# A Strassen-like combination moved one unit later in the MLP's last eighth but one

## The chip, the cores and the metric

The kernel runs on one core of a Trainium2 chip. Its time is the device time of one execution in microseconds, and the number compared is the median over several runs.

Five engines take part, each with a queue of its own that runs in order: TensorE (PE in the profile, with its weight loads as PEld), VectorE (DVE), ScalarE (ACT), GpSimd (POOL) and SyncE (SP). Matmuls write to accumulator banks in PSUM. VectorE and ScalarE read those banks, and a bank can be written for the next result once its last reader is done.

## The reference

A trunk of two layers on 256 positions of width 2048. Each layer is a mixing block (attention and gating) and then an MLP; the change lies in the MLP.

```python
for l in range(DEPTH):                       # DEPTH = 2
    ...                                      # norm, input projection, attention and gating, output projection, residual
    h2 = rms_norm(x, norm2_g[l])
    x = x + jnp.square(jax.nn.relu(h2 @ w_up[l])) @ w_down[l]     # 2048 -> 8192 -> 2048
return rms_norm(x, final_g)
```

## The kernel before

**Precision.** Weights are split: `hi` is the weight rounded to the faster matmul type (a copy on ScalarE, L167), `lo` the rest (a subtraction on VectorE, L177). Activations are split in the same way (`half`, `hs`, `shared`). A product is three matmuls: hi by hi, lo by hi, hi by lo (L400, L402, L404). The weights stream from memory in blocks of 128 x 1024; one block is one *unit*: one load by SP into a `raw` buffer (7 of them), one `hi` (6 buffers), one `lo` (6 buffers), and 24 matmuls on PE.

**Order.** A list `steps` holds the work of PE in order, written out by hand; the main loop goes through it and counts units in `done` (`now` in the helpers). At each step it first issues the `hi` for the unit five places ahead, then what has come due, then the `lo` for the unit four places ahead, then loads, and then the step's matmuls; what follows a finished column (`after`) is issued behind them. `soon(n, fn)` makes a piece of work due n units after the unit at which it is called. So a number in `soon` sets at which place of every engine's queue the work stands, and nothing reorders it later.

**The MLP.** The 8192 hidden columns are worked in eighths, e = 0 to 7. Round e of the loop (e = 0 to 8) holds the up projection of eighth e (16 units, result in `inner` and `half`) and the down projection of eighth e − 1. Part of the down projection's columns is done in groups of 512 by `fast`, a scheme of seven products in place of eight (Strassen's) over 2 x 2 blocks; each `fast` step counts as four units. The seven sums of a group gather over the eighths, and at the group's last round `combine` makes the four result blocks from them. The first group (g = 0, columns 0 to 511 of the output) keeps its seven sums in the four `aux` banks of PSUM over all rounds, but the seventh's earlier part, which is stored in memory and read back by POOL (L877).

For group 0, `combine(stage, 0, ..., o)` is issued in round 7, which is the last eighth but one of the down projection. It consists of:
- a copy of the first sum on ScalarE (L813),
- eight adds and subtractions of 128 x 256 on VectorE (L814 to L819, L821, L822), which read the aux banks,
- three units later four scalings on ScalarE (L827, in `scale`),
- six and seven units later two sets of four transposes on PE (L839, in `turn_back`), each followed one unit later by an add to the residual x on VectorE (L499, in `update`).

**The stretch around it.** Below, D0 to D7 are the eight units of the ordinary down projection in round 7. They do column pairs 8, 10, 12 and 14 (blocks of 128 columns), two units each. In this round the units use two banks in turn, `acc0` and `acc1`: pair 10 (D2, D3) and pair 14 (D6, D7) both use `acc0`, pairs 8 and 12 `acc1`. After pair 10 is finished, two operations on VectorE free `acc0`: L761 multiplies the bank by the norm factors in place, L499 adds it to x. E0 to E15 are the units of round 8, the last eighth's down projection, with all four banks.

The calls are counted from the unit n of group 0's second `fast` step in round 7. Up units follow at n + 4 to n + 10, D0 to D7 at n + 11 to n + 18, E0 at n + 19. `combine` at n + 14 is issued at D3, the unit before pair 10's `after`.

```python
LAST = (4, 6, 8, 10, 0, 2, 12, 14)          # L65: order of the column pairs in round 8
soon(17 + 2 * i, lambda c=c: rest_in(c))    # L880: pairs 12 and 14 into x, at D6 and E0
```

Of the kernel before, what the change touches and what calls it, by code (L numbers as in the profile page):

```python
# [90 lines left out]
def trunk(ctx: ExitStack, tc: tile.TileContext, layout, xT, consts, gains, w, b_sp, w_sp, out):  # L91
# [23 lines left out]
    stage, stage_one = ar[:, 2048:3840], ar[:, 3840:4096]  # L115
# [130 lines left out]
    def soon(delay, fn):  # L246

        due.append((now[0] + delay, fn))
# [258 lines left out]
    def layer(l, n1, n2, n3, last):  # L507
# [261 lines left out]
        def rest_in(c):  # L769
            y = rest_sums[:, c - 12:c - 10, :]  # L770
            vec.tensor_tensor(y, y, wide(n2.R2), op=OP.mult)
            vec.tensor_tensor(x[:, c:c + 2, :], x[:, c:c + 2, :], y, op=OP.add)
# [35 lines left out]
        def combine(place, c, banks, o=None):  # L808

            d1, d2, d3, d5, d7, d6, d4 = (place[:, 256 * n:256 * (n + 1)] for n in range(7))  # L810
            p1, p2, p3, p5, p7, p6, p4 = o or (d1, d2, d3, d5, d7, d6, d4)
            if o:
                act.activation(d1, p1, AF.Copy)  # L813
            vec.tensor_tensor(d2, d1, p2, op=OP.add)  # L814
            vec.tensor_tensor(d6, d1, p6, op=OP.add)
            vec.tensor_tensor(d7, d6, p7, op=OP.add)
            vec.tensor_tensor(d6, d6, p5, op=OP.add)
            vec.tensor_tensor(d3, d6, p3, op=OP.add)
            vec.tensor_tensor(d4, d7, d4, op=OP.subtract)  # L819
            if o:  # L820
                vec.tensor_tensor(d4, d4, p4, op=OP.subtract)  # L821
            vec.tensor_tensor(d7, d7, p5, op=OP.add)  # L822

            def scale():
                for tt, out in enumerate(((d2, d3), (d4, d7))):
                    for d in out:
                        act.activation(d, d, AF.Copy, scale=n2.r2[:, tt:tt + 1])  # L827

            soon(3, scale)
            wait = 6 if o else 7  # L830
            soon(wait, lambda: turn_back(c, d2, d4, banks[0]))
            soon(wait + (1 if o else 2), lambda: turn_back(c + 2, d3, d7, banks[1]))

        def turn_back(c, first, second, bank):
            ps = bank()
            for j in range(2):
                for tt, src in enumerate((first, second)):
                    o = j * S + tt * P
                    pe.transpose(ps[:, o:o + P], src[:, j * P:(j + 1) * P], ident)  # L839
            soon(1, lambda: update(n3, c, ps, False, last))  # L840
# [27 lines left out]
        def seventh_out(e, o):  # L868
            act.activation(stage_one, o[6], AF.Copy)  # L869
            put(e, 0, slice(0, 256))  # L870

        def first_done(e):
            def f(o):
                if e < 7:
                    soon(5, lambda: seventh_out(e, o))
                else:
                    soon(10, lambda: nc.gpsimd.dma_start(stage[:, 1536:1792], far[0]))  # L877
                    soon(14, lambda: combine(stage, 0, [aux_bank] * 2, o))
                    for i, c in enumerate((12, 14)):
                        soon(17 + 2 * i, lambda c=c: rest_in(c))  # L880
            return f
# [186 lines left out]
```

## Time and profile before

| | |
|---|---|
| median of 3 runs | 2035.05 us (2034.97 to 2035.65) |
| span of the profiled execution, first to last instruction | 2033.3 us |
| median less that span | 1.75 us |
| TensorE busy | 2018.3 us (99%) |
| VectorE busy | 1577.6 us (78%) |
| ScalarE busy | 1213.4 us (60%) |
| GpSimd busy | 156.7 us (8%) |
| memory traffic over the span | 205 GB/s |

For the profiled execution the profile gives the span and no other time; what lies around it is taken from the median. Times inside are microseconds from the span's start. A timeline row reads: start, duration, engine, line of the kernel, operation, output<-input, shapes, count, and in brackets the idle time of that engine just before it with what ended it. Where an instruction waits for several things, the profile names the one that came last; if that one had nothing to do with it, the true cause is another that came at about the same time.

### The profile page before, as it was taken

The numbers are of one execution on the slowest core, as the hardware profiler recorded it, in microseconds if no ns is written. First come the engines' busy times: TensorE is split into PE (matmuls) and PEld (weight loads), VectorE is DVE, ScalarE is ACT, GpSimd is POOL, SyncE is SP. The second block draws the span as 40 slices with busy tenths as digits, with TensorE's granted clock in tenths as the row PEclk, the third lists the DMA queues.
The fourth block names the chain that finished last, engine by engine and source line by source line (L and its number), as shares of the span: only waits on it lengthen the run. The fifth ranks groups of instructions, "written<-read, shape, count | busy, mean of one in ns | idle before, by whom it ended". The sixth has DMA issues, their size and how long they took to land.

```text
span 2033.3 us, 40721 instructions
## 1 busy us (share of the span) xinstructions
PE 2018.3 (99%) x16834; PEld 1979.1 (97%) x16834; DVE 1577.6 (78%) x1950; ACT 1213.4 (60%) x1613; POOL 156.7 (8%) x200
## 2 busy tenths in 40 slices
PE   9999999999999999999999999999999999999997
PEld 8998999999999999999989989999999999999997
DVE  7566766688888898998856667667888898888985
ACT  7565454666666666656545654556666666667654
POOL 0002300000001001100000032000000100010000
PEclk9999999999999999999999999999999999999998
DMA  8555556566677766875664555565676776778562
GB/s 326 192 167 166 187 187 205 169 232 209 211 228 236 244 218 201 243 222 198 204 214 159 169 184 187 187 203 179 215 223 213 230 234 217 230 221 261 184 213 81
DMA packets 126443, 419.27 MB, mean 206 GB/s; under 512 B 14128, under 2 KB 22064, under 8 KB 126256
## 3 DMA queue, kind: packets, MB, share of 16 engines
q1 hardware_dynamic: 110800, 389.86, 56.4%
q0 software_dynamic: 14304, 23.86, 6.7%
q8 instruction: 132, 2.16, 0.4%
q10 hardware_dynamic: 1152, 2.94, 0.4%
q14 instruction: 55, 0.45, 0.1%
HBM read 394.58 MB, written 22.02 MB: 205 GB/s over the span
## 4 chain that ended last, share of the span: by engine, by line
PE 95%; DVE 3%; ACT 1%; issue 1%; DMA 1%; ACTq 0%; DVEq 0%; SPq 0%
PE acc L402 23%; PE acc L400 23%; PE acc L404 23%; PE acc L461 3%; PE acc L460 3%; PE acc L459 3%; PE aux L430 3%; PE aux L432 3%; PE acc L433 3%; PE aux L433 3%; PE acc L432 3%; PE acc L430 3%; DVE lo L177 1%; ACT hi L167 1%; PE aux L693 0%
## 5 line engine op out<-in xcount | busy, mean ns | idle before, releaser
L167 ACT ACTIVATE hi<-raw 128x1024 fp32r<-128x1024 f32 (+1 forms) x817 | 836.2, 1051 | 497.9 <-DVE raw L219 231.2
L177 DVE TENSOR_TENSOR lo<-raw,hi 128x1024 fp32r<-128x1024 f32 (+1 forms) x817 | 964.1, 1213 | 155.1 <-ACT hi L167 151.7
L400 PE MATMUL acc<-hs,hi 128*128 128x256 f32 x2816 | 781.3, 277 | 0.0
L402 PE MATMUL acc<-hs,lo 128*128 128x256 f32 x2816 | 779.4, 277 | 0.2
L404 PE MATMUL acc<-hs,hi 128*128 128x256 f32 x2816 | 778.3, 276 | 0.0
L402 PEld LDWEIGHTS acc<-hs,lo 128*128 128x128 f32 x2816 | 528.7, 188 | 2.5 <-DVE lo L177 1.8
L400 PEld LDWEIGHTS acc<-hs,hi 128*128 128x128 f32 x2816 | 528.7, 188 | 0.3 <-issue 0.2
L404 PEld LDWEIGHTS acc<-hs,hi 128*128 128x128 f32 x2816 | 528.6, 188 | 0.0
L400 PE MATMUL acc<-half,hi 128*128 128x256 f32 x1344 | 372.1, 277 | 2.3 <-ACT hi L167 2.3
L402 PE MATMUL acc<-half,lo 128*128 128x256 f32 x1344 | 371.0, 276 | 0.0
L404 PE MATMUL acc<-half,hi 128*128 128x256 f32 x1344 | 371.0, 276 | 0.0
L400 PEld LDWEIGHTS acc<-half,hi 128*128 128x128 f32 x1344 | 252.3, 188 | 2.6 <-ACT hi L167 2.6
L402 PEld LDWEIGHTS acc<-half,lo 128*128 128x128 f32 x1344 | 252.3, 188 | 0.0
L404 PEld LDWEIGHTS acc<-half,hi 128*128 128x128 f32 x1344 | 252.2, 188 | 0.0
L866 POOL DMA_DIRECT2D far<-ar x92 | 74.7, 983 | 1159.9 <-ACT ar L869 607.0
L432 PE MATMUL acc<-lo,shared 128*128 128x256 f32 x384 | 106.4, 277 | 0.0
L433 PE MATMUL acc<-hi,shared 128*128 128x256 f32 x384 | 106.1, 276 | 0.0
L430 PE MATMUL acc<-hi,shared 128*128 128x256 f32 x384 | 106.1, 276 | 0.0
L459 PE MATMUL acc<-hi,hs 128*128 128x512 f32 x256 | 101.5, 397 | 0.1
L461 PE MATMUL acc<-hi,hs 128*128 128x512 f32 x256 | 100.6, 393 | 0.0
L460 PE MATMUL acc<-lo,hs 128*128 128x512 f32 x256 | 100.1, 391 | 0.3 <-DVE lo L177 0.3
L643 DVE TENSOR_TENSOR half<-ar,half 128x512 fp32r<-128x512 f32 x72 | 49.7, 691 | 62.1 <-ACT half L640 61.0
(163 smaller groups left out, 2560.2 us busy)
## 6 DMA issues: line engine op xcount, KB each, us to landing
raw<-in_w SPq DMA_DIRECT2D x731, 512.0 KB, 4.7
far<-ar POOLq DMA_DIRECT2D x60, 256.0 KB, 6.0
far<-ar POOLq DMA_DIRECT2D x32, 128.0 KB, 4.5
ar<-far POOLq DMA_DIRECT2D x12, 256.0 KB, 8.6
raw<-in_w SPq DMA_DIRECT2D x10, 256.0 KB, 5.2
x<-in_xT SPq DMA_DIRECT2D x7, 256.0 KB, 5.6
out<-x SPq DMA_DIRECT2D x7, 256.0 KB, 3.1
shared<-in_b_sp ACTq DMA_DIRECT2D x2, 512.0 KB, 7.8
```

What stands on the lines that cost most here:

```text
L167: act.activation(self.h[:, j * m:(j + 1) * m], self.raw[:, j * m:(j + 1) * m], AF.Copy)
L177: vec.tensor_tensor(lo[:, r], self.raw[:, r], self.h[:, r].bitcast(F32), op=OP.subtract)
L400: pe.matmul(o, lhsT=hi, rhs=xs[:, 0, :], start=(k0 + k == 0 and (two or cb == 0)), stop=False, skip_group_check=True)
L402: pe.matmul(o, lhsT=wt.lo[:, k, cb * P:(cb + 1) * P], rhs=xs[:, 0, :], start=False, stop=False, skip_group_check=True)
L404: pe.matmul(o, lhsT=hi, rhs=xs[:, 1, :], start=False, stop=last, skip_group_check=True)
L430: pe.matmul(o[n], lhsT=xh, rhs=hi, start=(p == 0 and k == 0 and n in fresh), stop=False, skip_group_check=True)
L432: pe.matmul(o[n], lhsT=xh, rhs=lo, start=False, stop=False, skip_group_check=True)
L433: pe.matmul(o[n], lhsT=xl, rhs=hi, start=False, stop=(n in last and p == 1 and k == 1), skip_group_check=True)
L459: pe.matmul(ps, lhsT=xh, rhs=hi, start=(k0 + k == 0), stop=False)
L460: pe.matmul(ps, lhsT=xh, rhs=lo, start=False, stop=False)
L461: pe.matmul(ps, lhsT=xl, rhs=hi, start=False, stop=(k0 + k == KC - 1))
L866: nc.gpsimd.dma_start(far[g][:, r], src, **({} if e == max(g, 1) else {"accum_op": OP.add}))
```

## The change

One number in `first_done`: the combination of group 0 comes due at 15 units after n, in place of 14. This holds for both layers.

```diff
                 else:
                     soon(10, lambda: nc.gpsimd.dma_start(stage[:, 1536:1792], far[0]))
-                    soon(14, lambda: combine(stage, 0, [aux_bank] * 2, o))
+                    soon(15, lambda: combine(stage, 0, [aux_bank] * 2, o))
                     for i, c in enumerate((12, 14)):
                         soon(17 + 2 * i, lambda c=c: rest_in(c))
```

It is now issued at D4, behind the `after` of pair 10. Its scalings, transposes and adds are due relative to it and move by one unit as well.

VectorE's queue in layer 0 around the combination, the earlier file's rows with − and the changed one's with +. The names in it: `aux` are the banks of the seven sums, `ar` the place where they are combined, `acc_11479` the bank `acc0` with pair 10.

```order
 L643 TENSOR_TENSOR shared<-ar,shared 128x2x256 x2
+L177 TENSOR_TENSOR lo<-raw,hi 128x1024
+L761 TENSOR_TENSOR acc_11479<-acc_11479,nR_3824 128x512
+L499 TENSOR_TENSOR x<-x,acc_11479 128x512
 L814 TENSOR_TENSOR ar<-ar,aux 128x256
 L815 TENSOR_TENSOR ar<-ar,aux 128x256
```

Further down in the same queue, at the end of the eight operations:

```order
 L821 TENSOR_TENSOR ar<-ar,aux 128x256
 L822 TENSOR_TENSOR ar<-ar,aux 128x256
-L177 TENSOR_TENSOR lo<-raw,hi 128x1024
-L761 TENSOR_TENSOR acc_11479<-acc_11479,nR_3824 128x512
-L499 TENSOR_TENSOR x<-x,acc_11479 128x512
 L177 TENSOR_TENSOR lo<-raw,hi 128x1024 x2
```

One `lo` (for D7) and the two operations that free `acc0` have passed from behind the eight operations to ahead of them; the next two `lo` (for E0 and E1) stand behind all of it as before.

ScalarE's queue at the same place, with the copy L813 and the four scalings L827:

```order
 L640 ACTIVATE shared<-ar 128x2x256 x2
-L167 ACTIVATE hi<-raw 128x1024
+L167 ACTIVATE hi<-raw 128x1024 x2
 L813 ACTIVATE ar<-aux 128x256
 L167 ACTIVATE hi<-raw 128x1024 x3
 L827 ACTIVATE ar<-ar,nr_3823 128x256 x4
-L167 ACTIVATE hi<-raw 128x1024 x3
+L167 ACTIVATE hi<-raw 128x1024 x2
 L285 ACTIVATE hs<-x,cols 128x256 x2
```

The copy and the scalings both stand one `hi` conversion later. On PE the two sets of transposes stand ahead of E2 and E3 where they stood ahead of E1 and E2; on VectorE the add of the first set moves behind one more `lo`, and that of the second behind one more `lo` and the work of the next finished pair. The queues of POOL and SP keep their order.

## The prediction

> **What bounds the kernel now.** I read the page's first two parts first, to see which engine sets the time.
>
> ```profile
> span 2033.3 us, 40721 instructions
> PE 2018.3 (99%) x16834; PEld 1979.1 (97%) x16834; DVE 1577.6 (78%) x1950; ACT 1213.4 (60%) x1613; POOL 156.7 (8%) x200
> PEclk9999999999999999999999999999999999999998
> ```
>
> TensorE is busy for 99% of the span at full clock until the last slice. Anything that doesn't make PE wait is therefore free, and a change that moves no matmul in number can only win what PE loses in waits. So the next view was the list of waits with PE as the one that waits (line waited for, total us, times, longest), and the one line of the weight loads' list that names VectorE's low halves in the MLP.
>
> ```profile
> PE acc L400 <- ACT hi L167: 2.3, 2, 1.1
> PE aux L321 <- DVE nr L347: 1.2, 1, 1.2
> PE aux L986 <- DVE warm L982: 1.1, 1, 1.1
> PE acc L460 <- DVE lo L177: 0.3, 1, 0.3
> PEld acc L402 <- DVE lo L177: 1.8, 8, 0.3
> ```
>
> The largest entry happens twice, once per layer. L321 is the final norm, L986 the start; neither is near the change. The eight L402 waits are at most 0.3 us each. The two L400 waits lie in these stretches (busy time and count by engine, then granted clock, DMA share, GB/s):
>
> ```profile
> 960.00:970.00 10.00, 8.86 (x79) 8.69 (x78) 9.86 (x13) 4.87 (x8) 0.00 (x0) 1.00 0.58 177
> 970.00:980.00 10.00, 10.00 (x91) 10.00 (x90) 8.52 (x11) 4.51 (x6) 0.00 (x0) 1.00 0.63 206
> 1960.00:1970.00 10.00, 8.86 (x79) 8.69 (x78) 9.83 (x17) 5.30 (x8) 0.00 (x0) 1.00 0.39 132
> ```
>
> Both hold 79 matmuls where the neighbour holds 91, and VectorE is at 98% in both. Now the timeline of PE around the two gaps:
>
> ```profile
> 961.42 0.28 PE L404 MATMUL acc<-half,hi 128*128 128x256 f32 x1
> 962.84 0.36 PE L400 MATMUL acc<-half,hi 128*128 128x256 f32 x1 [1.14 <-ACT hi L167]
> 963.03 0.28 PE L402 MATMUL acc<-half,lo 128*128 128x256 f32 x1
> 963.15 0.28 PE L404 MATMUL acc<-half,hi 128*128 128x256 f32 x1
> ...
> 1967.79 0.28 PE L404 MATMUL acc<-half,hi 128*128 128x256 f32 x1
> 1969.21 0.36 PE L400 MATMUL acc<-half,hi 128*128 128x256 f32 x1 [1.14 <-ACT hi L167]
> ```
>
> From start to start the gap is 1.42 us in both layers (962.84 − 961.42, 1969.21 − 1967.79), where the steady pace is 0.113 (10 us over the window's matmuls comes to 0.11; the ScalarE rows below give 2.72 us for 24). That is 1.31 lost, and the first matmul after the gap takes 0.19 to the next instead of 0.11: 1.39 us per layer. The count agrees: 12 missing matmuls times 0.113 are 1.36.
>
> **Who really ends that wait.** The profile names ScalarE's hi conversion. Here are ScalarE and then VectorE in layer 0 (start, us, engine, line):
>
> ```profile
> 947.35 2.00 ACT L167 ACTIVATE hi<-raw 128x1024 fp32r<-128x1024 f32 x2
> ...
> 954.55 0.36 ACT L813 ACTIVATE ar<-aux 128x256 f32<-128x256 f32 x1
> 956.30 1.07 ACT L167 ACTIVATE hi<-raw 128x1024 fp32r<-128x1024 f32 x1 [1.39 <-PE acc L404]
> 959.02 1.07 ACT L167 ACTIVATE hi<-raw 128x1024 fp32r<-128x1024 f32 x1 [1.65 <-PE acc L404]
> 961.74 1.06 ACT L167 ACTIVATE hi<-raw 128x1024 fp32r<-128x1024 f32 x1 [1.65 <-PE acc L404]
> 962.70 1.70 ACT L827 ACTIVATE ar<-ar,nr 128x256 f32<-128x256 f32 x4
> ```
>
> ```profile
> 954.66 1.22 DVE L177 TENSOR_TENSOR lo<-raw,hi 128x1024 fp32r<-128x1024 f32 x1
> 955.79 1.29 DVE L643 TENSOR_TENSOR shared<-ar,shared 128x512 fp32r<-128x512 f32 x2
> 957.00 0.41 DVE L814 TENSOR_TENSOR ar<-ar,aux 128x256 f32<-128x256 f32 x1
> ...
> 959.82 0.41 DVE L822 TENSOR_TENSOR ar<-ar,aux 128x256 f32<-128x256 f32 x1
> 960.15 1.22 DVE L177 TENSOR_TENSOR lo<-raw,hi 128x1024 fp32r<-128x1024 f32 x1
> 961.28 0.69 DVE L761 TENSOR_TENSOR acc<-acc,nR 128x512 f32<-128x512 f32 x1
> 962.01 0.69 DVE L499 TENSOR_TENSOR x<-x,acc 128x512 f32<-128x512 f32 x1
> 962.61 2.35 DVE L177 TENSOR_TENSOR lo<-raw,hi 128x1024 fp32r<-128x1024 f32 x2
> ```
>
> Each hi conversion waits for PE to finish a unit (released by L404, 2.72 us apart): with six hi buffers, the one at 961.74 refills the buffer of the unit that PE has just finished, D5, for a unit five places behind D6, E3. D6's own hi is the second conversion of the pair at 947.35, done at 949.35. It can't be what D6 waits for. What D6 does need is bank acc0, held by column pair 10 until L499 has read it; L499 ends at 962.01 + 0.69 = 962.70, 0.14 before D6's first matmul. D3, the last unit that wrote that bank, ended near 956.2 (its end releases the conversion at 956.30). The two freeing operations started five microseconds after that, because the eight operations of the combination and one lo stood ahead of them. ScalarE's name is coincidence: its conversion began with the same end of D5 and took 1.06.
>
> **The change, step by step.** Nothing is added or removed: the same instructions, five places in the queues.
>
> 1. VectorE. The eight operations L814 to L822 take 957.00 to 960.15, 3.15 us. They now come behind the lo, L761 and L499. The lo starts at 957.00, L761 at 958.13 (1.13 later, as 961.28 − 960.15), L499 at 958.86 (0.73 later) and ends at 959.55. PE would be ready for D6 at 961.42 + 0.11 = 961.53. Margin 1.98 us, so the wait goes entirely: −1.39 per layer. Lower bound of the gain: the 1.14 that the row itself counts as idle; upper bound 1.39, since PE can't be faster than its pace. I take 1.39, because the pace before and behind the gap is measured.
>
> 2. The combination itself runs from about 959.46 to 962.61, and the two lo behind it start at 962.61 as before: the queue only changed its order. These are for E0 and E1, ending about 963.8 and 964.96. PE, no longer held, reaches D7 at 964.25, E0 at 966.97 and E1 at 969.69 (steps of 2.72), so they are early by 3.1 and 4.7 us. These margins, shorter by 1.39 than before, are the next thing that could be late.
>
> 3. ScalarE. The copy L813 moves behind one hi. In place of 954.55 it starts about 0.97 after the conversion at 956.30, that is 957.27, and ends at 957.63; L814 now wants it at 959.46. Cover 1.8 us, from the work of step 1 on VectorE; without that cover the combination would be late one for one. The four scalings (1.70 us) move from behind E3's hi to behind E4's, which waits for the end of D6: 964.46 (961.53 + 2.72 + the 0.21 between a unit's last slot and its release), plus 0.97, to 967.1. E5's hi stands behind them and is released by D7's end at 967.18: no delay.
>
> 4. PE's transposes and their adds. The rows before, from the chain of work, and VectorE's first free moment after the stretch:
>
> ```profile
> 971.25 0.44 PE aux L839 x4
> 974.43 0.44 PE aux L839 x4
> 974.47 0.69 DVE L499 TENSOR_TENSOR x<-x,acc 128x512 f32<-128x512 f32 x1 [0.86 <-PE acc L404]
> ```
>
> The two sets go from ahead of E1 and E2 to ahead of E2 and E3, at the same 0.44 each on PE: zero. The first would start at 972.41, 5.3 us after the scalings end; that margin covers it. VectorE's backlog ends at 974.47, where it waits for PE again, and the adds of the transposed pairs come one unit later into a queue with room. Aux banks are free by then, with no other user before the next norm.
>
> 5. Queues moved past: SP and POOL keep their order. The combination issues no DMA; POOL's read of the stored seventh product, which it needs, stays at its count. SP's weight loads wait for lo to free a raw buffer; one lo comes 3.15 us earlier, none later. Zero, and no gain, as PE never waits for a landing here.
>
> Sum: 2 × 1.39 = 2.78 us. Layer 0's part survives to the end because PE is the chain there (no wait over 0.3 between the two places). The profiled span would be 2033.3 − 2.78 = 2030.5. The median is 1.75 above that span and keeps that distance: 2035.05 − 2.78 = 2032.27, called **2032.3 us**. By the lower bound, 2 × 1.14, it would be 2032.8. This is 0.14%; I take 0.2% (4.07 us) as what a measurement of this kernel tells from no change.
>
> **Clock.** Does the gap also cost clock? The row of 960 to 970 grants 1.00 and the matmuls after 963.03 come every 0.12, so here it doesn't. If the records hid a clock at half for one unit (24 matmuls, 2.72 us longer), each gap would be worth 4.11 and the time 2026.8. The Trainium skill, "TensorE: Matmul & The Clock Gate", section "A second HAM failure mode: psum-queue depth-cycling", says that short idles of TensorE while it cycles through accumulator banks can make the clock gate swing between half and full. By that rule the gain would be the larger one; the trace disagrees, with a granted clock of 1.00 across the gap.
>
> **Rivals.**
> - The profile's releaser is right and D6 waits for a hi conversion: the wait stays, 2035.05. For it: the conversion ends at 962.80, 0.04 before the matmul. Against it: the buffer count above. Chance 0.03.
> - Only part comes back, as a wait on one of the late lo of step 2, or in one layer: half, 2033.7. Against it: margins of 3.1 us and more. Chance 0.04.
> - Slower: the copy L813, now behind a conversion that waits for PE, holds the combination and with it E0's lo. PE begins to wait if L814 starts after 962.6 (966.97 − 3.15 − 1.22), and from 964.0 the layer is slower than before. It would take three conversions ahead of the copy instead of the one: behind D6's end at 964.46, copy done 965.9, E0's lo at 970.3, 3.3 lost against 1.39 won, 1.9 in each layer: 2038.9. Chance 0.03, for anything of this kind, as large or larger.
> - The clock rule: 2026.8, chance 0.02.
>
> **Numbers.** My forecast has 0.88. Range: below, the full gain and the 0.7 by which the three runs differ (2031.5); above, the lower bound and the same 0.7 (2033.5), stretched over the half gain to 2034.0. That leaves out no effect, slower and clock, 0.08, and what the runs may scatter beyond. Faster by over 0.2%: 0.03 (the clock case and scatter). Slower by over 0.2%: 0.03. The rest, 0.94, is within it, my forecast included: I expect a real gain that is too small for this measure.
>
> **What would show it.** Right: the entry L400 <- ACT hi is gone from PE's waits; D6 follows D5 at 0.11; about 91 matmuls in both windows; L499 of pair 10 ends some 2 us ahead of D6; lo of E0 still early. Wrong: the same gap with L499 done early (then hi was the cause); a new PE wait on lo at E0 to E3 or on ScalarE at the transposes; a span that falls by clearly more than 2.8.

## The result and the profile after

The changed kernel takes 2031.93 us (median of 21 runs, 2031.46 to 2032.44), the kernel before 2034.97 in the same series (21 runs, 2033.88 to 2035.65). The ratio is 0.9985 with a 95% interval of 0.9979 to 0.9991, which is 1.8 to 4.3 us won. Forecast were 2032.3 in a range of 2031.5 to 2034.0, and a time within 0.2% of before; both came out.

The profiled span falls from 2033.3 to 2030.5. First the list of PE's waits in the changed kernel (line waited for, total us, times, longest), in place of the one shown before:

```profile
PE aux L321 <- DVE nr L347: 1.2, 1, 1.2
PE aux L986 <- DVE warm L982: 1.1, 1, 1.1
PE acc L460 <- DVE lo L177: 0.5, 1, 0.5
```

The 2.3 us of L400 have gone and nothing of the change's place has come in. In the windows the 79 matmuls of both stretches have become 91, at the same granted clock (the column behind POOL):

```profile
960.00:970.00 10.00, 10.00 (x91) 10.00 (x90) 9.79 (x16) 5.11 (x8) 0.00 (x0) 1.00 0.48 160
...
1960.00:1970.00 10.00, 10.00 (x91) 10.00 (x90) 9.83 (x17) 3.94 (x5) 0.00 (x0) 1.00 0.35 111
```

VectorE is as busy as before; only its order is another. Its timeline in layer 0, where this execution runs 0.24 us later than the one before (0.07 of it since the start, the rest from a stretch at 925 to 931 in which its matmuls follow at 0.118 us in place of 0.113; the last section comes back to that):

```profile
957.24 1.22 DVE L177 TENSOR_TENSOR lo<-raw,hi 128x1024 fp32r<-128x1024 f32 x1
958.38 0.69 DVE L761 TENSOR_TENSOR acc<-acc,nR 128x512 f32<-128x512 f32 x1
959.10 0.69 DVE L499 TENSOR_TENSOR x<-x,acc 128x512 f32<-128x512 f32 x1
959.71 0.41 DVE L814 TENSOR_TENSOR ar<-ar,aux 128x256 f32<-128x256 f32 x1
...
962.86 2.35 DVE L177 TENSOR_TENSOR lo<-raw,hi 128x1024 fp32r<-128x1024 f32 x2
```

The bank is free at 959.10 + 0.69 = 959.79, and PE goes from D5 to D6 at its pace:

```profile
961.66 0.28 PE L404 MATMUL acc<-half,hi 128*128 128x256 f32 x1
961.78 0.28 PE L400 MATMUL acc<-half,hi 128*128 128x256 f32 x1
961.89 0.28 PE L402 MATMUL acc<-half,lo 128*128 128x256 f32 x1
```

The moved tail, on ScalarE and PE:

```profile
957.50 0.36 ACT L813 ACTIVATE ar<-aux 128x256 f32<-128x256 f32 x1
...
965.71 1.69 ACT L827 ACTIVATE ar<-ar,nr 128x256 f32<-128x256 f32 x4
```

```profile
972.66 0.60 PE L839 MATMUL aux<-con,ar 128*128 128x128 f32 x4
975.84 0.60 PE L839 MATMUL aux<-con,ar 128*128 128x128 f32 x4
```

The scalings end at 967.40, 5.3 us ahead of the first transposes, and no row of PE there shows a wait.

### The profile page after: what moved, and what is told of

Its sections match the earlier page's. It is cut to its first block, busy times and chain, and to the rows that moved or that the text cites. A ratio compares the mean times of both kernels' runs of the same rounds, so it can differ in the third digit from the quotient of the medians.

```text
span 2030.5 us, 40718 instructions
## 1 busy us (share of the span) xinstructions
PE 2017.7 (99%) x16834; PEld 1979.0 (97%) x16834; DVE 1577.2 (78%) x1950; ACT 1213.3 (60%) x1613; POOL 157.1 (8%) x200
## 4 chain that ended last, share of the span: by engine, by line
PE 95%; DVE 3%; ACT 1%; issue 1%; DMA 1%; ACTq 0%; DVEq 0%; SPq 0%
PE acc L402 23%; PE acc L400 23%; PE acc L404 23%; PE acc L461 3%; PE acc L459 3%; PE acc L460 3%; PE aux L430 3%; PE aux L432 3%; PE acc L432 3%; PE aux L433 3%; PE acc L433 3%; PE acc L430 3%; DVE lo L177 1%; ACT hi L167 0%; PE aux L693 0%
## 5 line engine op out<-in xcount | busy, mean ns | idle before, releaser
L400 PE MATMUL acc<-hs,hi 128*128 128x256 f32 x2816 | 781.2, 277 | 0.0
L400 PEld LDWEIGHTS acc<-hs,hi 128*128 128x128 f32 x2816 | 528.8, 188 | 0.4 <-issue 0.2
L400 PE MATMUL acc<-half,hi 128*128 128x256 f32 x1344 | 371.9, 277 | 0.0
L400 PEld LDWEIGHTS acc<-half,hi 128*128 128x128 f32 x1344 | 252.3, 188 | 0.0
```

The lines of the kernel that those rows point to most:

```text
L400: pe.matmul(o, lhsT=hi, rhs=xs[:, 0, :], start=(k0 + k == 0 and (two or cb == 0)), stop=False, skip_group_check=True)
```

## The experiments

The theory: D6 waits for bank `acc0`, which L499 of pair 10 frees, and the combination delays L499. Its first rival: D6 waits for ScalarE's hi conversion, as the profile had it. The second: the gain comes from the scalings and transposes that move along. Each comparison has its own runs of the kernel before on the same chip, 2035.48 us in the first four and 2034.82 in the last four. The lines of all kernels carry the same numbers, except that the split combination is one line (L820).

**Another bank, same queues.** Round 7's ordinary down units use four banks in place of two.

```diff
-                               apart=last and e == 8, of=2 if e < 8 else 4,
+                               apart=last and e == 8, of=2 if e < 7 else 4,
```

> The combination stays where it was before the change; in round 7 the ordinary down units use all four banks in turn, so that D6 writes a bank that nobody holds. No queue of VectorE or ScalarE changes. Bank theory (D6 waits for L499 of pair 10): the wait at D6 goes in both layers, span and time about 2.8 us under before, as with the change. Rival, the releaser that the profile names (ScalarE's hi conversion): the wait of 1.14 stays twice and the time is that of before.

2032.05 us against 2035.48, ratio 0.9986 (0.9976 to 0.9995): the gain of the change, with the combination where it was. VectorE still frees pair 10's bank late, in its row of that kernel:

```profile
962.23 0.69 DVE L499 TENSOR_TENSOR x<-x,acc 128x512 f32<-128x512 f32 x1
```

but D6 no longer needs it, and PE's list has no L400 wait:

```profile
PE aux L321 <- DVE nr L347: 1.2, 1, 1.2
PE aux L986 <- DVE warm L982: 1.1, 1, 1.1
PE acc L460 <- DVE lo L177: 0.5, 1, 0.5
```

ScalarE's queue has the same order as before, so a wait for a hi conversion would have stayed. It is the bank that D6 waits for.

**The conversion twice.** The kernel before, with E3's hi done twice.

```diff
-                act.activation(self.h[:, j * m:(j + 1) * m], self.raw[:, j * m:(j + 1) * m], AF.Copy)
+                for _ in range(2 if self in again else 1): act.activation(self.h[:, j * m:(j + 1) * m], self.raw[:, j * m:(j + 1) * m], AF.Copy)
...
-            quick = dict(quick)
+            quick = dict(quick); again.extend([down[3][0]] if e == 8 else [])
```

> The kernel before, with one more copy on ScalarE: the hi conversion of the unit E3, the one that the profile names as the releaser of D6, is done twice in a row, to the same values, 1.07 us more on ScalarE. Bank theory: D6 starts when it did, wait unchanged, time of before within 0.3 us, and the profile names another releaser or VectorE. Rival, the hi conversion is the releaser: D6 starts 1.07 us later in each layer, 2.1 us over before.

2035.08 us against 2035.48, ratio 0.9999 (0.9990 to 1.0008): no change. The rows of that kernel for VectorE, ScalarE and PE (its stretch runs 2.1 us later than in the kernel before, 0.2 since the start and most of the rest from 811 to 877, where its matmuls follow at 0.118 us; the differences count):

```profile
964.11 0.69 DVE L499 TENSOR_TENSOR x<-x,acc 128x512 f32<-128x512 f32 x1
```

```profile
963.84 2.15 ACT L167 ACTIVATE hi<-raw 128x1024 fp32r<-128x1024 f32 x2 [1.65 <-PE acc L404]
```

```profile
964.95 0.36 PE L400 MATMUL acc<-half,hi 128*128 128x256 f32 x1 [1.14 <-ACT hi L167]
```

D6 starts 0.15 after the end of L499 (964.80), as before, and a full microsecond ahead of the end of the second conversion (965.99). The profile goes on naming ScalarE, for the first of the two. I had expected it to name another: a wrong name can outlive its disproof.

**Tail alone, and head alone.** First only the scalings, transposes and adds one unit later (from the kernel before), then only the copy and the eight operations (from the changed one).

```diff
-            soon(3, scale)
-            wait = 6 if o else 7
+            soon(4 if o else 3, scale)      # tail alone
+            wait = 7 if o else 7
...
+            soon(2 if o else 3, scale)      # head alone
+            wait = 5 if o else 7
```

> The eight operations and the copy stay where they were before the change; only the scalings, the transposes and their adds come one unit later. Bank theory: the wait at D6 stays, time of before within 0.3 us. Rival, that the later tail brings the gain: about 2.8 us under before.

> The complement: the copy and the eight operations one unit later as in the change, the scalings, transposes and adds where they were before it. Bank theory: all of the gain, 2.8 us under before, no wait at D6; the scalings then follow the combination by a few tenths of a us and still end well ahead of the transposes. Rival, that the tail matters: the time of before.

Tail alone: 2035.74 against 2035.48, ratio 1.0001 (0.9992 to 1.0011), with the wait in place:

```profile
PE acc L400 <- ACT hi L167: 2.3, 2, 1.2
```

Head alone: 2031.79, ratio 0.9985 (0.9975 to 0.9994), the whole gain. The scalings then stand right behind the combination without harm. So the tail of the change is worth nothing in either direction, as its margins said.

**How much may stand ahead.** The combination is split after six, and after four, of its eight operations.

```diff
+            some(ops[:6] if o else ops)                   # or 4; at 14
+            soon(1, lambda: some(ops[6:] if o else []))   # at 15
```

> The combination is split: its copy and first six of the eight VectorE operations stay ahead of the bank's freeing, the last two come behind it; scalings and transposes one unit later as in the change. Bank theory: each operation ahead is 0.39 us (3.15 by 8), the margin is 1.98 less 0.14 from L499's end to PE, so six ahead leave 6 x 0.39 - 1.84 = 0.52 us of wait and 0.08 of restart in each layer: about 1.6 us under before. Rival (any releaser that isn't this queue): no wait as in the change, or the full one as before.

> The same with four ahead and four behind. Bank theory: 4 x 0.39 = 1.58 is under the margin of 1.84, so no wait at D6 and the change's full gain, 2.8 us under before. Rival, that any operation ahead costs in proportion: half of the gain, 1.4 us under before.

Six ahead, rows of VectorE, ScalarE and PE:

```profile
960.97 0.69 DVE L499 TENSOR_TENSOR x<-x,acc 128x512 f32<-128x512 f32 x1
```

```profile
961.48 1.06 ACT L167 ACTIVATE hi<-raw 128x1024 fp32r<-128x1024 f32 x1 [1.65 <-PE acc L404]
```

```profile
961.16 0.28 PE L404 MATMUL acc<-half,hi 128*128 128x256 f32 x1
961.80 0.36 PE L400 MATMUL acc<-half,hi 128*128 128x256 f32 x1 [0.36 <-DVE x L499]
962.00 0.28 PE L402 MATMUL acc<-half,lo 128*128 128x256 f32 x1
```

The gap is 0.64 from start to start, 0.53 more than the pace, and 0.09 of restart: 0.62, where 0.52 and 0.08 were expected. And here, where E3's conversion ends only at 962.54, behind D6's start, the profile names L499 itself. The wait came out as forecast, the time did not: the medians, 2033.87 against 2034.82, are 0.95 us apart where 1.6 was expected, ratio 0.9996 (0.9987 to 1.0005), which can't be told from no change nor from the expected gain. (The profiled execution, with a span 1.8 below before, was the fastest of the ten.) The trace shows a cost that the forecast left out. Behind the wait the matmuls follow at 0.118 in place of 0.113, at full granted clock, until the transposes; 10 us hold 86 where the rows of the changed kernel above hold 91:

```profile
962.00:972.00 10.00, 10.00 (x86) 10.00 (x86) 9.86 (x12) 5.33 (x8) 0.00 (x0) 1.00 0.72 235
```

```profile
973.19 0.60 PE L839 MATMUL aux<-con,ar 128*128 128x128 f32 x4
```

From D6's first matmul to the transposes it is 11.39 us (961.80 to 973.19) against 10.88 in the changed kernel (961.78 to 972.66): 0.51 more, restart included. With the gap's 0.53 that is 1.04 per layer, which leaves 2 x (1.39 − 1.04) = 0.7 of the gain, near the 0.95 measured. Four ahead gives 2031.68, ratio 0.9985 (0.9976 to 0.9994), without any L400 wait; L499 ends at 961.10, 0.4 ahead of D6's slot at its pace:

```profile
960.41 0.69 DVE L499 TENSOR_TENSOR x<-x,acc 128x512 f32<-128x512 f32 x1
```

The ten runs of the two kernels don't overlap (2033.29 to 2034.47 with six, 2031.37 to 2032.06 with four). The cost is a threshold and not proportional: nothing up to the margin; beyond it the wait grew one for one, and the slower matmuls behind it came on top.

**The next margin.** The changed kernel with twelve more operations in the combination, to the same values.

```diff
-            vec.tensor_tensor(d2, d1, p2, op=OP.add)
+            for _ in range(13 if o else 1): vec.tensor_tensor(d2, d1, p2, op=OP.add)
```

> The changed kernel with the combination's first add done thirteen times in a row, to the same values: twelve more operations of 128x256 on VectorE behind the freed bank. It measures the margin of the next thing that could be late, the lo of E0 (3.1 us by the prediction). At 0.33 to 0.45 us each the twelve are 4.0 to 5.4 us: beyond 3.1 PE waits 0.9 to 2.3 us in each layer for lo at E0 or E1, 1.8 to 4.6 us over the changed kernel. Rival, that the prefetched lo buffers hide it: no wait, the changed kernel's time.

2038.14 us, ratio 1.0016 (1.0007 to 1.0025) to the kernel before and 6.2 over the changed kernel's series, above the 4.6 that was expected at most. VectorE and PE:

```profile
959.38 5.88 DVE L814 TENSOR_TENSOR ar<-ar,aux 128x256 f32<-128x256 f32 x13
965.17 0.41 DVE L815 TENSOR_TENSOR ar<-ar,aux 128x256 f32<-128x256 f32 x1
...
967.99 2.35 DVE L177 TENSOR_TENSOR lo<-raw,hi 128x1024 fp32r<-128x1024 f32 x2
```

```profile
966.88 0.28 PE L400 MATMUL acc<-half,hi 128*128 128x256 f32 x1
969.26 0.39 PE L402 MATMUL acc<-half,lo 128*128 128x256 f32 x1 [2.10 <-DVE lo L177]
```

The thirteen take 5.79 us from start to start of what follows, 5.46 more than the one. PE loses 2.38 − 0.11 = 2.27 at E0's second matmul, so 3.19 us were hidden: the margin that step 2 put at 3.1. Twice 2.27 is 4.5, and the restart, 0.12 each (0.23 to the next matmul in place of 0.11), makes it 4.8; the time rose by more. The windows, of layer 0 and then of layer 1, say why (granted clock in the column after POOL):

```profile
966.00:969.00 3.00, 1.16 (x11) 0.96 (x9) 2.90 (x7) 1.73 (x4) 0.00 (x0) 1.00 0.00 0
969.00:972.00 3.00, 2.74 (x15) 2.74 (x16) 2.93 (x5) 0.63 (x1) 0.00 (x0) 0.67 0.57 169
972.00:975.00 3.00, 3.00 (x23) 3.00 (x22) 3.00 (x4) 1.06 (x1) 0.00 (x0) 0.76 0.73 206
975.00:978.00 3.00, 3.00 (x29) 3.00 (x28) 2.93 (x5) 0.00 (x0) 0.00 (x0) 1.00 0.83 285
...
1978.00:1981.00 3.00, 2.92 (x25) 2.92 (x26) 2.93 (x5) 0.45 (x1) 0.00 (x0) 1.00 0.60 198
```

Behind the wait of layer 0 the granted clock is below full in two windows; at half, that is 2 x (0.33 + 0.24) x 3 = 3.4 us, and the matmuls there follow at 0.21. Behind the equal wait of layer 1 it stayed full. The same work, from the first matmul behind the wait to the transposes, shows the price:

```profile
976.34 0.60 PE L839 MATMUL aux<-con,ar 128*128 128x128 f32 x4
...
1978.08 0.39 PE L402 MATMUL acc<-half,lo 128*128 128x256 f32 x1 [2.10 <-DVE lo L177]
...
1983.53 0.60 PE L839 MATMUL aux<-con,ar 128*128 128x128 f32 x4
```

It took 7.08 us in layer 0 (969.26 to 976.34) and 5.45 in layer 1 (1978.08 to 1983.53): the clock cost 1.6. With the 4.8 that is 6.4, near the 6.2 measured.

**One unit more.** The combination due at 16.

```diff
-                    soon(15, lambda: combine(stage, 0, [aux_bank] * 2, o))
+                    soon(16, lambda: combine(stage, 0, [aux_bank] * 2, o))
```

> The combination one further unit later (due at 16). Bank theory: no wait before, so nothing to win; D7, E0 and E1 get their lo as early or earlier, the transposes go ahead of E3 and E4: the changed kernel's time within 0.3 us. Rival, that lateness itself keeps paying: faster than the changed kernel by another 1 us or more.

2031.74 us, ratio 0.9985 (0.9975 to 0.9995): the same as at 15. Lateness pays once, by clearing the wait. Five kernels (the change, four banks, head alone, four ahead, sixteen) thus lie between 2031.7 and 2032.1, and none beats the others.

## Why the prediction was right

- **Who ends the wait.** The buffer count said L499 against the profile's ScalarE. Four banks removed the wait with both queues untouched; a conversion twice as long didn't move D6. Shown.
- **Size, step 1.** 1.39 per layer. Two marks of the traces before and after check it. The next layer's norm starts at 1024.78 before and 1023.63 after, 1.15 earlier, and with the 0.24 by which the changed execution ran later ahead of D6 that is 1.39. From layer 1's L798 to its last 128x512 L499, 1956.02 to 2013.93 before, 1954.67 to 2011.20 after, the stretch is shorter by 1.38. The forecast of the freed bank (959.55, and the same 0.24) agrees with 959.79.
- **Steps 2 to 4.** E0's and E1's lo start at 962.86 (forecast 962.61 + 0.24), the copy at 957.50 (957.27 + 0.24), the scalings end at 967.40 (967.1 + 0.24), the transposes stand at 972.66 (972.41 + 0.24). One reading was off: VectorE's backlog, which ended at 974.47 before, doesn't end there after, as PE now arrives earlier than it:

```profile
973.77 0.68 DVE L499 TENSOR_TENSOR x<-x,acc 128x512 f32<-128x512 f32 x1
975.03 0.88 DVE L289 SCALAR_TENSOR_TENSOR hs<-x,cols,hs 128x256 fp32r<-128x256 f32 x2 [0.58 <-ACT hs L285]
```

  Its 0.86 of idle was part of the slack that PE's 1.39 used up. With lo four units ahead this cost nothing.
- **Sum.** 2.78 was forecast; the spans give 2.8. The series of 21 runs gives 3.0, with 2.78 within its interval. What the further 0.26 are isn't shown; one execution differs from another by more than that. In the ten profiles the first norm's L321 starts between 51.06 and 52.15, and the stretches of slower matmuls differ as well (last section).
- **Clock.** The two gaps of 1.3 us had no price in clock: full in both windows before, and the gain is the gap's own length with its restart. The clock rule that was weighed there did not show with two idles of 1.1 us in a span of 2033 us. Behind one of the two waits of 2.1 us in the twelve-more run the clock did drop, as the last section tells.
- **What the forecast didn't weigh.** It took a wait to cost its length and 0.08 of restart, and no more. For the gaps of this change that came out; the run with six operations ahead shows that a shorter wait can cost 0.4 more in each layer by slower matmuls behind it. The rows behind the two gaps of the kernel before show none of that.

## What to carry over

When a profile puts a wait on an engine, count the buffers: if that engine's result belongs to a unit several places ahead, its end only falls at the same time, and the true releaser has to be looked for among the other operations that ended just then (here VectorE's L499, 0.1 us earlier). To test it, give the waiter another bank, or lengthen the named operation, each with the rest of the queues as they are. And in a kernel bound by one engine, order a loaded side queue by what the bound engine needs next; a long piece that nobody wants for five units belongs behind two short ones that free a bank, and moving it further earns nothing.

## What I had not expected of the hardware

A wait of PE of 2.1 us, 2.38 from one matmul's start to the next, halved the granted clock for 3.4 us in one layer and left it full in the other, in the same execution. The ten runs of that kernel lie in three groups, 2036.2 to 2036.5 (three), 2037.9 to 2038.7 (six) and 2040.4 (one), about 2 apart. None, one or two half-clock stretches of 1.6 each would come near that, and the profiled execution, with one, is of the middle group; but only that one was profiled. The Trainium skill, "TensorE: Matmul & The Clock Gate", section "What's actually happening", gives about 3.4 us as the length of a free-running activity window and an idle window as what throttles; the length of the slow stretch agrees here, but a gap clearly shorter than the window was enough once. The gaps of 1.1 us idle, two each in the profiles of the kernel before, the tail alone and the conversion twice, cost no clock in any of the six places.

The second thing is a slower pace of the matmuls at full granted clock: 0.118 us from one to the next in place of 0.113. It stands longest in the profile of the conversion twice, with short breaks from 811.04 to 876.88, about 2.2 us lost; in this window the kernel before holds 90 matmuls and that one 88 (before, then the conversion twice):

```profile
830.00:840.00 10.00, 10.00 (x90) 10.00 (x89) 7.62 (x8) 8.56 (x12) 2.70 (x3) 1.00 0.78 232
830.00:840.00 10.00, 10.00 (x88) 10.00 (x87) 6.87 (x7) 7.83 (x11) 2.70 (x3) 1.00 0.76 232
```

This stretch, the one in the changed kernel (924.82 to 930.94) and the two of six ahead begin right behind a hold of PE of 0.1 to 0.5 us over its pace, and each is over at a set of transposes. But not every hold is followed by it: in the kernel before, the same hold at the place of 924.82 is followed by less than 1 us of it, and the waits of 1.14 us there and of 2.10 us in layer 1 of the twelve-more run by none. What decides it isn't shown. It makes executions of one kernel differ by 2 us and more, so a difference of two single spans is to be read only with the pace in both.
